# Second product of the MLP: another set of seven half-size products, with sums of the weights made in DRAM

## The chip, the cores and the metric

The program runs on one NeuronCore of a Trainium2 chip. The metric is device time in microseconds, from runs of the whole program; the profile comes from one more execution. TensorE multiplies, VectorE (DVE), ScalarE (ACT) and GpSimd (POOL) work on tiles of 128 partitions, and SyncE (SP) only issues DMA transfers.

## The reference

One layer of an encoder on 1024 tokens of width 1024 in float32: stick-breaking attention with 16 heads, an output projection and LayerNorm; cross-attention of 4 heads into 256 memory rows, a projection and LayerNorm; and a gated MLP:

```python
def conv_ffn(h, w_up, conv_w, conv_b, w_down):
    u = h @ w_up
    ch = u.shape[-1]
    u = lax.conv_general_dilated(u, conv_w, window_strides=(1,), padding=((CONV_W - 1, 0),),
                                 dimension_numbers=('NWC', 'WIO', 'NWC'), feature_group_count=ch) + conv_b
    g, val = jnp.split(u, 2, axis=-1)
    return (jax.nn.gelu(g) * val) @ w_down
```

`w_up` is 1024 x 5632 and `w_down` 2816 x 1024. A LayerNorm of 2^0.25 h plus this is the output. The change is in the last product, `@ w_down`.

## The kernel before

Each float32 matrix product is made of three TensorE products (`mm3`, L98 to L101): an operand x is kept as a high half, x rounded to the type float32r (a copy, most often on ScalarE, L77), and a low half, x minus that (a subtraction on VectorE, L83, or GpSimd, L85); high x high, high x low and low x high are added in a PSUM bank. `split` (L75) makes the halves.

The stages in order of time: attention with the q, k and v projections (to about 560 us), the first output projection and LayerNorm (`out_ln`, first loop of eight row blocks), cross-attention, the second output projection and LayerNorm (`out_ln`, second loop), the first product of the MLP with convolution and gate, whose gated rows are stored transposed in DRAM (`g_d`, 22 tiles of 128 channels x 1024 tokens), and the second product with the last LayerNorm.

At the very start x is loaded (`xT`, L392) in 16 pieces of 256 KB through two buffers (`sig`), split, and multiplied with the weights of the first head; `weights` (L162 to L168) loads and splits those of the next heads. In attention GpSimd makes low halves (L81, L85, L135, L136) and a mask (L217) that stands before VectorE's scan (L220).

The second product is cut in two along each of its three dimensions: tokens (th), channels (kh) and output columns (nh), so each quarter is 512 tokens x 1408 channels x 512 columns, with 11 = `NH` tiles of 128 channels. Seven half-size products replace the eight, from sums of the quarters (`plans`, L784 to L790): each product m has a sum of gated quarters and a sum of weight quarters. Products 2 and 4 run together, then 6 and 1, each pair in all eight banks, and then 3, 5, 7 one after the other in four banks each. For each of the 11 tiles `operands2` (L840) loads the blocks it needs, adds them on VectorE (L836), and splits them: the gated side with ScalarE and VectorE, the weight side with ScalarE and GpSimd. `plus` (L861) adds the finished banks and the residual into the output quarters; `finish` (L867) does a LayerNorm of 128 rows and stores them.

The program is written in one order, but a planner at build time (`schedule_with_timeline_sim=True`) sets the order of each engine's and queue's instructions; it keeps the dependencies through tiles and their buffers.

Of the kernel before, what the change touches and what calls it, by code (L numbers as in the profile page):

```python
# [19 lines left out]
F32 = mybir.dt.float32  # L20
# [15 lines left out]
NFF = 22  # L36
ALPHA = 2.0 ** 0.25
# [3 lines left out]
def trunk(ctx, tc, out, xT, xn, memT, wqk, wv, wo, xq, xk, xv, xo, up, cw, dn, lng, lnb):  # L41
# [17 lines left out]
    vm_d = dram.tile([P, 2, D], F32, name="vm_d")  # L59
    h1_d = [dram.tile([P, D], F32, name=f"h1_d{i}") for i in range(NTB)]  # L60
# [608 lines left out]
    with ExitStack() as c3:  # L669
# [3 lines left out]
        for i in range(NTB):  # L673
            out_ln(i, i, o2_d, wts2, h1_d, rp, gb, h2_d, h2_evac, first_products if i == NTB - 1 else None)
# [91 lines left out]
    for p in range(2, len(seq) - 1):  # L766
# [5 lines left out]
        else:  # L772
# [9 lines left out]

    NH = NFF // 2
    plans = {1: (("11", "22", ALU.add), ("11", "22", ALU.add)),  # L784
             2: (("21", "22", ALU.add), ("11",)),
             3: (("11",), ("12", "22", ALU.subtract)),
             4: (("22",), ("21", "11", ALU.subtract)),
             5: (("11", "12", ALU.add), ("22",)),
             6: (("21", "11", ALU.subtract), ("11", "12", ALU.add)),
             7: (("12", "22", ALU.subtract), ("21", "22", ALU.add))}  # L790
    with ExitStack() as c4:
        ea = c4.enter_context(pool(name="ea", bufs=1, reuse_waits="tile"))
        ep = c4.enter_context(pool(name="ep", bufs=1, reuse_waits="tile"))
        g_raw = {}

        def g_block(n, kt):
            th, kh = int(n[0]) - 1, int(n[1]) - 1
            if (n, kt) not in g_raw:
                if n == "21":
                    t = ea.tile([P, 512], F32, name="g21", bufs=NH + 2)  # L800
                elif n == "11":
                    if kt % 2 == 0:
                        g_raw["pair"] = ep.tile([P, 2, 512], F32, name="g11", bufs=6)
                    t = g_raw["pair"][:, kt % 2]
                else:
                    t = (ea if n == "22" and kt < 4 else ep).tile([P, 512], F32, name=f"g{n}_{kt}")
                g_raw[n, kt] = t
                nc.sync.dma_start(out=t, in_=g_d[NH * kh + kt][:, 512 * th:512 * th + 512])
            return g_raw[n, kt]

        w_kept, w_free = {}, []

        def w_blocks(ns, kt):

            ts = {}
            for n in ns:
                if n == "22":
                    if kt in w_kept:
                        ts[n] = w_kept[kt]
                        continue  # L820
                    t = w_kept[kt] = ea.tile([P, 512], F32, name="g21", bufs=NH + 2)
                else:
                    if not w_free:
                        pair = wrawp.tile([P, 2, 512], F32, name="wraw")
                        w_free.extend((pair[:, 0], pair[:, 1]))
                    t = w_free.pop(0)
                ts[n] = t
                kh, nh = int(n[0]) - 1, int(n[1]) - 1
                nc.sync.dma_start(out=t, in_=dn[NH * kh + kt][:, 512 * nh:512 * nh + 512])
            return ts  # L830

        def operand(plan, blocks, d, lo):
            x = blocks[plan[0]]
            if len(plan) > 1:
                t = ea.tile([P, 512], F32, name="sum", bufs=4)
# [155 lines left out]
```

## Time and profile before

| | us |
|---|---|
| median of 3 runs | 1615.63 (1611.7 to 1618.11) |
| the profiled execution | 1616.26 |
| its span, first to last instruction | 1614.5 |
| TensorE busy | 1524.7 (94%) |
| VectorE busy | 1162.7 (72%) |
| ScalarE busy | 705.2 (44%) |
| GpSimd busy | 730.4 (45%) |
| mean granted clock of TensorE | 0.984 |

All times of the rows are microseconds from the first instruction of that execution. PE is TensorE's matmuls, PEld its weight loads, SPq the DMA issues of SyncE. A matmul's own time of some 390 ns overlaps its neighbours'; what counts is how many there are in a stretch.

### The profile page before, as it was taken

What the parts mean: (1) busy time and instruction counts of PE and PEld (TensorE: products, weight loads), DVE (VectorE), ACT (ScalarE), POOL (GpSimd) and SP (SyncE); (2) the same over time, 40 slices, a digit from 0 to 9 for tenths busy, and PEclk for the clock granted to TensorE, in tenths of its full rate; (3) what the DMA queues carried; (4) which work ended last, traced back from release to release, by engine and by line L of the source; (5) the groups of instructions that cost most, each with busy time, mean ns of one, the idle gap of its engine ahead of it and who ended that gap; (6) DMA issues with size and microseconds to landing.
All of it is one profiled execution on the core that took longest, in us unless ns stands there. A gap on an engine that the chain in (4) does not pass through costs nothing.

```text
span 1614.5 us, 20972 instructions
## 1 busy us (share of the span) xinstructions
PE 1524.7 (94%) x7508; PEld 1262.0 (78%) x7508; DVE 1162.7 (72%) x1494; ACT 705.2 (44%) x1320; POOL 730.4 (45%) x604
## 2 busy tenths in 40 slices
PE   7999999999988999999999799999999998998975
PEld 5888888888877888888888577888888886866753
DVE  3466666666689556564467898777777778899998
ACT  4554655655676411233322444444444444433432
POOL 5865565656577601465002333232322234445584
PEclk9999999999999999999999999999999999999988
DMA  5322222222247433243253122222222216743221
GB/s 168 93 56 63 64 55 63 69 56 61 65 136 231 133 117 126 97 129 110 68 182 125 54 92 79 86 88 87 79 80 90 79 60 241 281 146 121 72 88 69
DMA packets 86520, 167.93 MB, mean 104 GB/s; under 512 B 10000, under 2 KB 31632, under 8 KB 86416
## 3 DMA queue, kind: packets, MB, share of 16 engines
q1 hardware_dynamic: 78352, 148.76, 29.0%
q10 hardware_dynamic: 8064, 17.83, 3.4%
q8 instruction: 59, 0.97, 0.3%
q14 instruction: 45, 0.37, 0.1%
HBM read 123.56 MB, written 34.60 MB: 98 GB/s over the span
## 4 chain that ended last, share of the span: by engine, by line
PE 71%; DVE 14%; issue 4%; DMA 4%; POOL 4%; ACT 2%; SPq 1%; DVEq 0%; POOLq 0%; ACTq 0%
PE yacc L99 4%; PE yacc L100 4%; PE yacc L101 4%; PE tp L229 3%; PE qkacc L101 3%; PE qkacc L99 3%; PE qkacc L100 3%; PE mb L99 3%; PE mb L101 3%; PE mb L100 3%; DVE sum L836 3%; PE ma L99 2%; PE ma L100 2%; PE mc L101 2%; PE mc L99 2%
## 5 line engine op out<-in xcount | busy, mean ns | idle before, releaser
L85 POOL TENSOR_TENSOR whl<-wraw,whl 128x512 fp32r<-128x512 f32 (+2 forms) x108 | 189.4, 1764 | 188.9 <-ACT whl L77 186.1
L220 DVE TENSOR_TENSOR_SCAN sig<-sig 128x896 f32<-128x896 f32 (+7 forms) x128 | 196.2, 1539 | 74.8 <-POOL sig L217 53.8
L83 DVE TENSOR_TENSOR wT<-tp,wT 128x512 fp32r<-128x512 f32 (+1 forms) x160 | 98.9, 629 | 64.2 <-ACT wT L77 63.1
L77 ACT CAST wT<-tp 128x512 fp32r<-128x512 f32 (+1 forms) x160 | 86.5, 545 | 104.9 <-PE tp L229 100.9
L100 PE MATMUL y<-whl,aop 128*128 128x512 f32 x292 | 118.1, 407 | 12.9 <-POOL whl L85 12.7
L101 PE MATMUL y<-whl,aop 128*128 128x512 f32 x292 | 114.8, 400 | 4.4 <-DVE aop L83 4.4
L99 PE MATMUL mb<-b_t,ws 128*128 128x512 f32 x264 | 105.0, 398 | 10.2 <-ACT ws L77 8.2
L215 ACT ACTIVATE sig<-z 128x384 f32<-128x384 f32 (+2 forms) x192 | 92.1, 496 | 51.4 <-PE z L214 50.2
L217 POOL TENSOR_SCALAR_AFFINE_SELECT sig<-sig 128x128 f32<-128x128 f32 x128 | 59.1, 466 | 119.5 <-ACT sig L215 111.8
L85 POOL TENSOR_TENSOR whl<-sum,whl 128x512 fp32r<-128x512 f32 x51 | 83.1, 1642 | 66.4 <-ACT whl L77 64.0
L99 PE MATMUL qkacc<-xh,whl 128*128 128x512 f32 x256 | 102.8, 402 | 8.2 <-POOL whl L85 5.6
L99 PE MATMUL y<-whl,aop 128*128 128x512 f32 x292 | 93.4, 405 | 11.8 <-ACT whl L77 6.6
L101 PE MATMUL mb<-b_t,ws 128*128 128x512 f32 x264 | 103.9, 395 | 0.0
L100 PE MATMUL mb<-b_t,ws 128*128 128x512 f32 x264 | 103.8, 393 | 0.0
L101 PE MATMUL qkacc<-xh,whl 128*128 128x512 f32 x256 | 101.1, 396 | 1.8 <-POOL whl L85 1.8
L100 PE MATMUL qkacc<-xl,whl 128*128 128x512 f32 x256 | 101.3, 396 | 0.0
L100 PE MATMUL yacc<-wo,whl 128*128 128x512 f32 x256 | 100.9, 394 | 0.0
L99 PE MATMUL yacc<-wo,whl 128*128 128x512 f32 x256 | 100.5, 393 | 0.3 <-ACT whl L77 0.3
L101 PE MATMUL yacc<-wo,whl 128*128 128x512 f32 x256 | 100.6, 394 | 0.0
L229 PE MATMUL tp<-ident,sig 128*128 128x128 f32 x576 | 89.4, 275 | 9.3 <-DVE wT L83 9.3
L77 ACT CAST ws<-wt 128x512 fp32r<-128x512 f32 x88 | 54.3, 620 | 93.3 <-PE mb L101 49.6
L81 POOL TENSOR_SCALAR whl<-wraw 128x512 fp32r<-128x512 f32 (+2 forms) x74 | 54.8, 753 | 88.0 <-PE qkacc L101 32.1
(224 smaller groups left out, 4416.3 us busy)
## 6 DMA issues: line engine op xcount, KB each, us to landing
wraw<-in_dn SPq DMA_DIRECT2D x66, 256.0 KB, 3.0
wraw<-in_up SPq DMA_DIRECT2D x22, 512.0 KB, 3.7
wr<-in_up SPq DMA_DIRECT2D x22, 512.0 KB, 3.5
g_d<-gate SPq DMA_DIRECT2D x22, 512.0 KB, 2.6
g<-g_d SPq DMA_DIRECT2D x44, 256.0 KB, 5.4
q<-q SPq DMA_DIRECT2D x64, 128.0 KB, 2.2
h_d<-r SPq DMA_DIRECT2D x32, 256.0 KB, 2.1
wraw<-in_wqk SPq DMA_DIRECT2D x15, 512.0 KB, 3.6
```

The lines of the kernel that those rows point to most:

```text
L77: nc.scalar.copy(out=hi, in_=src)
L81: nc.gpsimd.tensor_scalar(out=hi, in0=src, scalar1=1.0, scalar2=0.0, op0=ALU.mult, op1=ALU.add)
L83: nc.vector.tensor_tensor(out=lo, in0=src, in1=hi.bitcast(F32), op=ALU.subtract)
L85: nc.gpsimd.tensor_tensor(out=lo, in0=src, in1=hi.bitcast(F32), op=ALU.subtract)
L99: nc.tensor.matmul(o, lhsT=lh, rhs=rh, start=first, stop=False, skip_group_check=more)
L100: nc.tensor.matmul(o, lhsT=lh, rhs=rl, start=False, stop=False, skip_group_check=more)
L101: nc.tensor.matmul(o, lhsT=ll, rhs=rh, start=False, stop=last, skip_group_check=more)
L215: nc.scalar.activation(out=sig[:, a:b], in_=z[:, :b - a], func=AF.Sigmoid, scale=-0.125)
L217: nc.gpsimd.affine_select(out=sig[:, S - P:S], in_=sig[:, S - P:S], pattern=[[-1, P]], base=-1, channel_multiplier=1, compare_op=ALU.is_ge ...
L220: nc.vector.tensor_tensor_scan(out=kr, data0=kr, data1=kr, initial=1.0, op0=ALU.mult, op1=ALU.bypass)
L229: nc.tensor.transpose(out=tp[:, k], in_=sigs[2 * d + u][:, P * j:P * j + P], identity=ident)
L836: nc.vector.tensor_tensor(out=t, in0=x, in1=blocks[plan[1]], op=plan[2])
```

## The change

The second product uses another scheme of seven products with four sums on each side. With A for the gated quarters (first index tokens, second channels) and B for the weights' (channels, columns), the weights' sums are u1 = B11 + B12, u3 = B22 + B12, u2 = B22 + u1, u4 = B21 + u2. They are not made in SBUF: `u_steps` first copies 44 blocks of 256 KB from DRAM to DRAM on SyncE's queue, and then adds 44 blocks into them with accumulating transfers issued by GpSimd. Its steps are written six after each row block of the first output projection, and six before each of the second.

The gated quarters are loaded once into tiles of their own (`slot`, 4 x 11 blocks) and summed in place. The products come one by one, 1, 6, 2, 7, 5, 4, in two sets of four banks that alternate; products 2, 7 and 4 go on in banks that hold an earlier product. Each factor has its high half from ScalarE and its low half from VectorE. During products 5 and 4 the halves for the last product (slot 2 and B22) are made and kept, and that product is run row block by row block at the end with a LayerNorm behind each; the four LayerNorms of the other token half don't depend on it.

The diff, without the lines that it removes from the second product's stage (they are in the kernel above):

```diff
@@ -34,6 +34,7 @@
 M = 256
 XH = 4
 NFF = 22
+NH = NFF // 2
 ALPHA = 2.0 ** 0.25
 EPS = 1e-5
@@ -57,6 +58,7 @@
     o2_d = [[dram.tile([P, n, P], F32, name=f"o2_d{i}_{n}") for n in (6, 2)] for i in range(NTB)]
     km_d = [dram.tile([P, M], F32, name=f"km_d{i}") for i in range(KT)]
     vm_d = dram.tile([P, 2, D], F32, name="vm_d")
+    u_d = {n: [dram.tile([P, 512], F32, name=f"{n}_d{i}") for i in range(NH)] for n in ("u1", "u2", "u3", "u4")}
     h1_d = [dram.tile([P, D], F32, name=f"h1_d{i}") for i in range(NTB)]
     h2_d = [dram.tile([P, D], F32, name=f"h2_d{i}") for i in range(NTB)]
@@ -409,6 +411,23 @@
         pass
+    def b_block(n, kt):
+        kh, nh = int(n[0]) - 1, int(n[1]) - 1
+        return dn[NH * kh + kt][:, 512 * nh:512 * nh + 512]
+    def u_steps():
+        for n, x in (("u1", "11"), ("u3", "22"), ("u2", "22"), ("u4", "21")):
+            for kt in range(NH):
+                nc.sync.dma_start(out=u_d[n][kt], in_=b_block(x, kt))
+                yield
+        for n, x in (("u1", "12"), ("u3", "12"), ("u2", "u1"), ("u4", "u2")):
+            for kt in range(NH):
+                nc.gpsimd.dma_start(out=u_d[n][kt], in_=u_d[x][kt] if x[0] == "u" else b_block(x, kt),
+                                    accum_op=ALU.add, max_dma_last_dim=2048)
+                yield
     def load_ln(p, n):
         g = p.tile([P, D], F32, name="lng", bufs=1)
         b = p.tile([P, D], F32, name="lnb", bufs=1)
@@ -481,11 +500,14 @@
     def h1_evac(i, c, tp):
         split(tp, h1h[:, 4 * c:4 * c + 4, P * i:P * i + P], h1l[:, 4 * c:4 * c + 4, P * i:P * i + P])
+    u_sums = u_steps()
     with ExitStack() as c1:
         lnp = c1.enter_context(pool(name="ln1", bufs=1, side="right", reuse_waits="tile"))
         gb = load_ln(lnp, 0)
         for k, i in enumerate((4, 5, 2, 3, 0, 1, 6, 7)):
             out_ln(k, i, o_d, wts, xn, state["rp"], gb, h1_d, h1_evac)
+            for _ in range(6):
+                next(u_sums, None)
     mem_c.close()
@@ -671,6 +693,8 @@
         rp = c3.enter_context(pool(name="rp2", bufs=2, reuse_waits="tile"))
         gb = load_ln(lnp, 1)
         for i in range(NTB):
+            for _ in range(6):
+                next(u_sums, None)
             out_ln(i, i, o2_d, wts2, h1_d, rp, gb, h2_d, h2_evac, first_products if i == NTB - 1 else None)
@@ -780,176 +804,140 @@
...
+    plan = {1: (0, "11"), 6: (0, "u2"), 2: (2, "21"), 7: (None, "u3"), 5: (1, "u1"), 4: (3, "u4")}
     with ExitStack() as c4:
         ea = c4.enter_context(pool(name="ea", bufs=1, reuse_waits="tile"))
         ep = c4.enter_context(pool(name="ep", bufs=1, reuse_waits="tile"))
...
+        rs = [ep.tile([P, D], F32, name=f"y{i}") for i in range(NTB)]
+        slots = {}
+        def room(kt, s, dt):
+            return (ea if kt < 5 else ep).tile([P, 512], dt, name=f"{dt.name}{s}_{kt}", tag=f"g{s}_{kt}", bufs=1)
+        def slot(kt, s):
+            if (kt, s) not in slots:
+                t = slots[kt, s] = room(kt, s, F32)
+                nc.sync.dma_start(out=t, in_=g_d[NH * (s // 2) + kt][:, 512 * (s % 2):512 * (s % 2) + 512])
+            return slots[kt, s]
+        w_free = []
+        def w_block(n, kt):
+            if not w_free:
+                pair = wrawp.tile([P, 2, 512], F32, name="wraw")
+                w_free.extend((pair[:, 0], pair[:, 1]))
+            t = w_free.pop(0)
+            nc.sync.dma_start(out=t, in_=u_d[n][kt] if n[0] == "u" else b_block(n, kt))
+            return t
         def rows(n):
             th, nh = int(n[0]) - 1, int(n[1]) - 1
             return [(4 * th + b, slice(512 * nh, 512 * nh + 512)) for b in range(4)]
...
         quarters = {n: [rs[i][:, ns] for i, ns in rows(n)] for n in ("11", "12", "21", "22")}
...
+        c11, c12, c21, c22 = (quarters[n] for n in ("11", "12", "21", "22"))
+        def residual(n, b, x, op=ALU.add):
             i, ns = rows(n)[b]
...
+            t = ea.tile([P, 512], F32, name="h2r", bufs=2)
             nc.sync.dma_start(out=t, in_=h2_d[i][:, ns])
...
+            nc.vector.scalar_tensor_tensor(out=quarters[n][b], in0=t, scalar=ALPHA, in1=x, op0=ALU.mult, op1=op)
+        def add(d, x, y):
+            nc.vector.tensor_tensor(out=d, in0=x, in1=y, op=ALU.add)
+        def finish(i, spread):
+            layer_norm((rs[i][:, 0:512], rs[i][:, 512:1024]), *gb, spread=spread)
             for n in range(2):
                 ns = slice(512 * n, 512 * n + 512)
                 (nc.scalar if n else nc.sync).dma_start(out=out[i, :, ns], in_=rs[i][:, ns])
...
+        def factors(m, kt):
+            s, n = plan[m]
+            if m == 6:
+                nc.vector.tensor_tensor(out=slot(kt, 0), in0=slot(kt, 1), in1=slot(kt, 0), op=ALU.subtract)
+            if m == 7:
+                x = ea.tile([P, 512], F32, name="sum", bufs=2)
+                nc.vector.scalar_tensor_tensor(out=x, in0=slot(kt, 0), scalar=-1.0, in1=slot(kt, 3),
+                                               op0=ALU.mult, op1=ALU.subtract)
+            else:
+                x = slot(kt, s)
+            w = w_block(n, kt)
+            a = ea.tile([P, 2, 512], R, name="aop", bufs=4)
+            if kt % 2 == 0:
+                two["w"] = whlp.tile([P, 2, 2, 512], R, name="whl")
+            return (x, (a[:, 0], a[:, 1])), (w, (two["w"][:, kt % 2, 0], two["w"][:, kt % 2, 1]))
+        two = {}
+        def down(bank, b, a, w, first, last, more):
             bb = slice(P * b, P * b + P)
...
+            mm3(bank, a[0][:, bb], a[1][:, bb], w[0], w[1], first, last, more)
+        banks = ([f(name="ya") for f in (acc_tile, acc_tile, pv_tile, pv_tile)],
+                 [f(name="yb") for f in (z_tile, z_tile, tp_tile, tp_tile)])
+        last_ops = [[None, None] for _ in range(NH)]
+        gb = None
+        for n, m in enumerate((1, 6, 2, 7, 5, 4)):
+            y = banks[n % 2]
+            more = m in (2, 7, 4)
+            if m == 5:
+                y = banks[0][:] = [f(name="ya") for f in (acc_tile, acc_tile, pv_tile, pv_tile)]
             for kt in range(NH):
...
+                ops = factors(m, kt)
+                for x, d in ops:
+                    split(x, *d)
+                a, w = ops[0][1], ops[1][1]
+                for b in range(4):
+                    down(y[b], b, a, w, kt == 0 and not more, kt == NH - 1, more)
+                if m == 1:
+                    nc.vector.tensor_tensor(out=slot(kt, 1), in0=slot(kt, 1), in1=slot(kt, 3), op=ALU.subtract)
+                if m == 2:
+                    add(slot(kt, 2), slot(kt, 2), slot(kt, 0))
+                if m == 5:
+                    t = w_block("22", kt)
+                    wo = room(kt, 0, R), room(kt, 1, R)
+                    split(t, *wo)
+                    last_ops[kt][1] = wo
                     if 3 <= kt < 7:
...
+                        residual("22", kt - 3, c22[kt - 3], ALU.subtract)
+                if m == 4:
+                    vo = room(kt, 3, R), room(kt - 1, 2, R) if kt else ea.tile([P, 512], R, name="vl")
+                    split(slot(kt, 2), *vo)
+                    last_ops[kt][0] = vo
+                    if 3 <= kt < 7:
+                        residual("21", kt - 3, c21[kt - 3])
                     elif kt >= 7:
...
+                        residual("12", kt - 7, c12[kt - 7], ALU.subtract)
+            if m == 7:
+                gb = load_ln(ep, 2)
             for b in range(4):
...
+                if m == 1:
+                    nc.scalar.copy(out=c21[b], in_=y[b])
+                elif m == 6:
+                    add(c12[b], y[b], c21[b])
+                elif m == 2:
+                    residual("11", b, y[b])
+                elif m == 7:
+                    add(c22[b], y[b], c21[b])
+                elif m == 5:
+                    add(c22[b], c22[b], y[b])
                 else:
...
+                    add(c21[b], c21[b], y[b])
+        for b in range(4):
             for kt in range(NH):
...
+                a, w = last_ops[kt]
+                down(banks[0][b], b, a, w, False, kt == NH - 1, True)
+            finish(4 + b, b < 3)
+            add(c12[b], c12[b], banks[0][b])
+            finish(b, b % 2 == 0)
 def kernel(**inputs):
```

## Rows read from the trace of the kernel before

**Rows 1.** Windows: in the first product, all of the second, 40 us of it.

```profile
1060.00:1100.00 40.00, 40.00 (x175) 32.61 (x174) 30.45 (x37) 18.21 (x24) 11.03 (x6) 1.00 0.23 79
1336.00:1615.00 279.00, 230.44 (x938) 178.11 (x936) 255.94 (x296) 104.15 (x182) 152.19 (x99) 0.94 0.42 143
1420.00:1460.00 40.00, 34.97 (x144) 25.87 (x142) 39.28 (x45) 13.08 (x23) 16.19 (x12) 1.00 0.47 143
```

**Rows 2.** Timeline: start us, us, engine, line, operation, names; first and last.

```profile
1336.58 0.50 PE L99 MATMUL y<-whl,aop 128*128 128x512 f32 x1 [0.22 <-ACT aop L77]
...
1596.75 0.39 PE L101 MATMUL y<-g,aop 128*128 128x512 f32 x1
...
1609.47 1.40 DVE L441 SCALAR_TENSOR_TENSOR y<-y,rs,lnb 128x512 f32<-128x512 f32 x2
```

**Rows 3.** Waits from 1338 us: total us, times, longest.

```profile
POOL whl L85 <- ACT whl L77: 101.3, 36, 11.2
ACT aop L77 <- DVE sum L836: 76.0, 27, 6.2
...
PE y L100 <- POOL whl L85: 12.7, 13, 3.1
```

**Rows 4.** Durations ns, min/median/max, of VectorE's operations in the second product.

```profile
L836 DVE TENSOR_TENSOR sum<-g,g x55: 636/680/1783, 1334.9 to 1586.1; 128x512 f32<-128x512 f32 x55
...
L863 DVE TENSOR_TENSOR y<-y,y x24: 632/674/692, 1426.3 to 1597.6; 128x512 f32<-128x512 f32 x24
L865 DVE SCALAR_TENSOR_TENSOR y<-sum,y x16: 669/1775/1798, 1424.4 to 1531.6; 128x512 f32<-128x512 f32 x16
```

**Rows 5.** Timeline within the second product.

```profile
1421.45 0.62 ACT L77 CAST aop<-sum 128x512 fp32r<-128x512 f32 x1 [3.62 <-DVE sum L836]
...
1422.67 2.99 POOL L85 TENSOR_TENSOR whl<-sum,whl 128x512 fp32r<-128x512 f32 x2 [2.40 <-ACT whl L77]
1422.84 1.68 DVE L836 TENSOR_TENSOR sum<-g,g 128x512 f32<-128x512 f32 x1
...
1426.86 0.68 DVE L836 TENSOR_TENSOR sum<-wraw 128x512 f32<-128x512 f32 x1
...
1427.46 0.68 DVE L83 TENSOR_TENSOR aop<-sum,aop 128x512 fp32r<-128x512 f32 x1
```

**Rows 6.** Timeline of SyncE's queue: loads of the second product.

```profile
1371.75 5.53 SPq L808 DMA_DIRECT2D g<-g_d  x9
1377.65 0.33 SPq L415 DMA_DIRECT2D lng<-in_lng  x1
```

**Rows 7.** Windows: the two output projections, the start, and attention.

```profile
561.00:660.00 99.00, 99.00 (x464) 81.98 (x464) 60.06 (x99) 14.85 (x22) 14.54 (x12) 1.00 0.36 119
820.00:905.00 85.00, 82.10 (x384) 67.28 (x383) 65.83 (x109) 25.75 (x45) 17.98 (x14) 0.99 0.38 130
0.00:30.00 30.00, 23.15 (x90) 17.79 (x91) 12.03 (x17) 11.21 (x17) 11.80 (x23) 1.00 0.65 210
30.00:60.00 30.00, 27.13 (x121) 21.18 (x120) 7.87 (x7) 14.33 (x28) 26.56 (x27) 1.00 0.31 88
100.00:150.00 50.00, 50.00 (x282) 42.80 (x281) 30.87 (x36) 27.77 (x62) 34.67 (x35) 1.00 0.27 75
```

**Rows 8.** Timeline of SyncE's queue at the start; landing of the x loads.

```profile
15.89 0.33 SPq L164 DMA_DIRECT2D wraw<-in_wqk  x1
...
17.89 7.12 SPq L392 DMA_DIRECT2D sig<-in_xT  x4
...
DMA to landing us min/median/max: 2.5/3.8/7.1
```

**Rows 9.** Timeline of ScalarE and GpSimd in attention.

```profile
129.13 0.20 ACT L148 COPY vend<-vT 128x4 f32<-128x4 f32 x1
...
129.85 0.12 POOL L144 MEMSET vT<- 128x1 f32 x1
```

**Rows 10.** Page, DMA issues: KB each, median us from issue to landing.

```profile
g<-g_d SPq DMA_DIRECT2D x44, 256.0 KB, 5.4
```

More of the change, by code (lines that the diff above doesn't have):

```diff
@@ L778, in trunk @@
     b4c.close()
[L783 to L790, printed above, removed]
+    plan = {1: (0, "11"), 6: (0, "u2"), 2: (2, "21"), 7: (None, "u3"), 5: (1, "u1"), 4: (3, "u4")}
     with ExitStack() as c4:
@@ L793, in trunk @@
         ep = c4.enter_context(pool(name="ep", bufs=1, reuse_waits="tile"))
[L794 to L835, printed above, removed]
-                nc.vector.tensor_tensor(out=t, in0=x, in1=blocks[plan[1]], op=plan[2])
-                x = t
-            split(x, d[:, 0], d[:, 1], "act", lo)
-        def operands2(ms, kt, a, w):
-            need = [sorted({n for m in ms for n in plans[m][s] if isinstance(n, str)}) for s in range(2)]
-            gs, ws = {n: g_block(n, kt) for n in need[0]}, w_blocks(need[1], kt)
-            for k, m in enumerate(ms):
-                operand(plans[m][0], gs, a[k], "dve")
-                operand(plans[m][1], ws, w[k], "pool")
+        rs = [ep.tile([P, D], F32, name=f"y{i}") for i in range(NTB)]
@@ L849, in rows @@
             return [(4 * th + b, slice(512 * nh, 512 * nh + 512)) for b in range(4)]
-        rs = [ep.tile([P, D], F32, name=f"y{i}") for i in range(NTB)]
         quarters = {n: [rs[i][:, ns] for i, ns in rows(n)] for n in ("11", "12", "21", "22")}
-        def residual(n, b):
+        c11, c12, c21, c22 = (quarters[n] for n in ("11", "12", "21", "22"))
+        def residual(n, b, x, op=ALU.add):
             i, ns = rows(n)[b]
-            t = ea.tile([P, 512], F32, name="sum", bufs=4)
+            t = ea.tile([P, 512], F32, name="h2r", bufs=2)
             nc.sync.dma_start(out=t, in_=h2_d[i][:, ns])
-            return t
-        def plus(n, b, x, y, op=ALU.add, scale=None, eng=None):
-            if scale is None:
-                (eng or nc.vector).tensor_tensor(out=quarters[n][b], in0=x, in1=y, op=op)
-            else:
-                nc.vector.scalar_tensor_tensor(out=quarters[n][b], in0=x, scalar=scale, in1=y, op0=ALU.mult, op1=op)
-        def finish(i):
-            layer_norm((rs[i][:, 0:512], rs[i][:, 512:1024]), *gb, spread=i in (0, 1, 4, 6))
+            nc.vector.scalar_tensor_tensor(out=quarters[n][b], in0=t, scalar=ALPHA, in1=x, op0=ALU.mult, op1=op)
[3 more added lines that the diff above has]
+            layer_norm((rs[i][:, 0:512], rs[i][:, 512:1024]), *gb, spread=spread)
             for n in range(2):
@@ L883, in trunk @@
-        banks = [acc_tile, acc_tile, pv_tile, pv_tile, z_tile, z_tile, tp_tile, tp_tile]
-        for ms in ((2, 4), (6, 1)):
-            ys = [[f(name="y") for f in banks[4 * k:4 * k + 4]] for k in range(2)]
-            for kt in range(NH):
-                a, w = operand_tiles()
-                operands2(ms, kt, a, w)
-                for k in range(2):
-                    for b in range(4):
-                        down(ys[k], b, a[k], w[k], kt)
-                if ms == (6, 1):
-                    if 3 <= kt < 7:
-                        b = kt - 3
-                        plus("22", b, residual("22", b), c21[b], ALU.subtract, ALPHA)
-                        plus("21", b, c21[b], c11[b])
+        def factors(m, kt):
[13 more added lines that the diff above has]
+            return (x, (a[:, 0], a[:, 1])), (w, (two["w"][:, kt % 2, 0], two["w"][:, kt % 2, 1]))
```

59 lines of the change are left out of this document (removed).

## The prediction

> **What bounds the kernel now.** I read the windows first, to find the stage that the change rewrites and what it lacks. Up to about 1336 us the first product of the MLP keeps TensorE full: 40.00 us busy in 40, 175 matmuls of 512 columns, so one per 0.2286 us [rows 1]. In the second product TensorE falls to 34.97 us in 40 while VectorE stands at 39.28, and over the whole of it VectorE is busy 255.94 us of 279 [rows 1]. The timeline gives the ends: the second product's first matmul starts at 1336.58 us, its last ends at 1597.14, and the last LayerNorm instruction ends at 1610.87, 3.6 us before the span of 1614.5 is over [rows 2]. This stage holds 7 products x 11 k-tiles x 4 row blocks x 3 = 924 matmuls and the 12 last ones of the first product. At 0.2286 us these 936 need 214.0 us; they took 260.5. So 46.5 us are lost inside the stage, and 17.4 us lie between the last matmul and the end of the span. That is all the change can win here.
>
> The waits say why: GpSimd waited 101.3 us for ScalarE and ScalarE 76.0 us for VectorE's sums, and TensorE's longest sum of waits is on GpSimd [rows 3]. VectorE is not full of work but of waiting for GpSimd: the same 128x512 sum takes 0.68 us at the median and 1.78 at most, and the residual's 1.78 at the median where 0.67 is the least [rows 4]. The timeline shows when: two GpSimd splits ran from 1422.67 to 1425.66, and the sum that VectorE started beside them took 1.68 us; once GpSimd was idle, VectorE took 0.68 us an operation and started one every 0.60 [rows 5].
>
> **The stage after the change.** GpSimd gets no split and no addition any more; it keeps the power of each LayerNorm and the products of five of them. VectorE gets 11 x (12 low halves of the six products + 4 sums + 2 low halves kept for the last product) = 198 operations. At 0.60 us each [rows 5] that is 119 us; 20 additions of banks at 0.67 are 13 and 16 residuals at 0.67 are 11 [rows 4]. Together 143 us, beside the 792 matmuls of the first six products, 181 us. A single product needs at most 33 x 0.60 + 8 x 0.67 + 4 x 0.67 = 28 us of VectorE against 132 x 0.2286 = 30.2 us of TensorE. ScalarE has 154 high halves at 0.62 us [rows 5], 95 us. So TensorE becomes the bound, and two bank sets give every evacuation a whole product of time.
>
> Not all of the 46.5 us come back. The first product's loads are four blocks of 256 KB a k-tile (three of gated rows, one of weights). The queue issued nine such loads in 5.53 us [rows 6], so a k-tile takes about 2.5 us of loading and 2.74 us of matmuls: just enough, with no reserve, and the rows from k-tile 5 on wait for buffers that the first product of the MLP frees, as the loads of this row did, sent at 1371.75 us. I leave 8 us lost (bounds 3 and 14: nothing but the first operands, or the whole of this row's load time paid twice). The tail: after the last matmul come one addition, one LayerNorm and the store. Four LayerNorms that do not wait for the last product and three that do are done under its 30 us of matmuls; a LayerNorm is at most six operations of VectorE on 512 columns, 4.1 us at 0.68, so seven and the additions are up to 32 us, and VectorE may end a little late. I take 13 us in place of 17.4 (bounds 9 and 17). Gain of the stage: 46.5 - 8 + 4.4 = 43 us, bounds 33 to 51.
>
> **The 44 copies and 44 accumulating transfers.** They are written beside the two output projections, where the DMA engines are 0.36 and 0.38 busy and TensorE is full or nearly so [rows 7]. There 44 copies at 0.61 us would fill 27 us of 184 and cost nothing; TensorE's work in these 184 us hides them, and if that cover were gone the price would be those 27 us. But they would have to stay there. They read weights that lie in DRAM from the start, and no buffer holds them back. The trace shows what happens to such work: queues are not filled in the order of the program. The weights of the second head were issued at 15.89 us, ahead of the last loads of the x that the first head still needs [rows 8]. The last LayerNorm's scale was fetched at 1377.65 us, in the middle of the first pair of products, though it is written after the second pair [rows 6]. A GpSimd memset ran at 129.85 us, right after the copy that ended at 129.33 and freed its buffer, and well ahead of its user [rows 9]. Each went as soon as its buffer was free. A copy that needs no buffer is free at 0 us.
>
> So I expect the 44 copies in the gaps of SyncE's queue in the first 40 us, and the accumulating transfers on GpSimd soon behind them. There the gaps exist (the four loads at 17.89 us spread over 7.12 us, with a buffer awaited between them [rows 8]), but the loads are on the path: x comes in through two buffers, so after the first two k-tiles there are three rounds, each waiting for its buffer and then for its load, and TensorE is already working (23.15 us of the first 30 [rows 7]). A full queue has a load land 5.4 us after its issue at the median, with issues 0.61 us apart, about eight in flight [rows 6, 10]. The x loads landed after 3.8 us [rows 8]. With copies in front, each round pays 5.4 - 3.8 plus 0.6 for its place: 2.2 us if copies go at the pace of loads, and at half that pace (they read and write DRAM, which no row shows) 10.8 - 3.8 + 1.2 = 8.2. Three rounds: 7 to 25 us; I take 16, the middle.
>
> The Trainium skill, "DMA: Bandwidth & Descriptors", section Latency and other measured facts, has DRAM-to-DRAM copies at up to 214 GB/s a direction; by that, 256 KB takes 1.2 us (an estimate), the half pace, and the price would be the upper 25 us rather than 16.
>
> GpSimd's part: it is busy 26.56 us of the 30 between 30 and 60 us, and 34.67 of 50 later [rows 7]. Behind an accumulating transfer stand its splits of q and k and the mask before VectorE's scan, and so the transposes on TensorE. No row has such an issue; the nearest are GpSimd's own, from 0.12 us (a memset [rows 9]) to 1.5 (a split [rows 5]). Hidden in its idle time it costs 0, at 44 x 1.5 all on the path 66. I take 9: a dozen fall where GpSimd is full, at 0.75 us. Later ones lie under TensorE's 50.00 us in 50. Price together 25 us, bounds 0 and 91.
>
> **Sum.** 1614.5 - 43 + 25 = 1596.5 us of span. The profiled execution took 1616.26, 1.8 more than its span and 0.6 more than the median of the runs, so the run should take about 1598 us.
>
> **The rivals.**
> *The copies cost nothing* (they stay at the projections, or the start has room): 1616.3 - 43 = 1573 us, 1565 to 1583. For it speaks that the DMA engines are only 0.65 busy in the first 30 us [rows 7]; against it [rows 8] and [rows 9].
> *The accumulating transfers hold GpSimd, and the kernel gets slower.* GpSimd's queue is in order: a transfer that has to wait for its copy, or for the one before it, stops the masks and splits of attention behind it. Place: 15 to 200 us. It decides once they put more than 43 - 16 = 27 us on the path, 0.6 us for each of the 44. At one 1.5 us operation each, 66 us, the run takes 1616.3 - 43 + 16 + 66 = 1655 us; at two thirds of that, 1633. For it: GpSimd has 3 us free between 30 and 60. Against: TensorE is full at 100 to 150 us although GpSimd is 0.69 busy [rows 7], so there is slack.
> The Trainium skill, "SBUF — State Buffer", section SBUF: two separate sides, warns of just this engine: transfers issued by GpSimd are held up while VectorE has the port that they share. By its figures, 3.1 us in place of 0.62, the 44 would take 136 us of GpSimd; no run here shows one yet.
> *VectorE stays the bound* (its operations stay at 1.0 us without GpSimd beside them): 198 + 25 + 8 LayerNorms of 4 us is 255 us, as much as now [rows 1]; gain 5, and with the 25 us of the start 1636 us. Against it stand the 0.60 us steps of [rows 5].
>
> **How the numbers follow.** My forecast (gain 33 to 51, price 12 to 40) has 0.50 and lies within 1578 and 1620, about 1598. Free copies 0.28; GpSimd's block 0.15; VectorE 0.07. A change of 0.5%, 8 us, is about what a measurement of this kernel tells from none: 1607.5 and 1623.7 are the bounds. Faster: 0.36 of my case, all 0.28, 0.01 of the rest, 0.65. Same: 0.13 and 0.05, 0.18. Slower: 0.01 and 0.16, 0.17. The range runs from inside the free case to the mild end of the block, 1566 to 1628.
>
> **What would show it.** Right: no GpSimd split and VectorE at 0.68 us in the last 280 us, TensorE at 39 us or more in 40, the last LayerNorm alone behind the last matmul; copies on SyncE's queue before 45 us, x landing later than 7 us, TensorE idle there by some 15 us more. Wrong: copies beside the projections (then near 1573), TensorE waiting for rows or weights in the stage, or attention stretched by GpSimd.

## Result: slower by 1.3%, and the profile after

The changed kernel takes 1636.43 us (median of 4 runs, 1633.92 to 1641.42) against 1615.78 before: ratio 1.0134, 95% interval 1.0103 to 1.0166. The profiled execution's span is 1634.6 us, 20.1 more than before. The forecast was 1598.

The stage that was rewritten did what it should. Windows of the changed kernel (us, then busy time and count of PE, PEld, DVE, ACT, POOL, the granted clock, the busy share of the DMA engines, GB/s): the start, then the whole second product and its first part.

```profile
0.00:30.00 30.00, 19.13 (x72) 14.40 (x72) 9.84 (x13) 8.72 (x13) 15.81 (x28) 1.00 0.90 270
30.00:60.00 30.00, 14.62 (x39) 10.04 (x40) 5.53 (x8) 8.53 (x17) 17.44 (x22) 0.61 1.09 277
60.00:100.00 40.00, 17.43 (x68) 13.73 (x67) 0.69 (x1) 5.91 (x10) 23.07 (x25) 0.71 1.09 253
100.00:150.00 50.00, 41.03 (x215) 34.45 (x216) 32.78 (x27) 22.31 (x50) 40.95 (x44) 0.85 0.63 143
1393.00:1635.00 242.00, 217.84 (x948) 178.86 (x948) 186.73 (x300) 98.61 (x166) 19.93 (x18) 0.96 0.49 163
1400.00:1420.00 20.00, 12.34 (x55) 9.84 (x53) 16.45 (x21) 5.41 (x7) 0.00 (x0) 0.89 0.64 219
1420.00:1440.00 20.00, 18.01 (x71) 14.74 (x72) 15.81 (x26) 8.43 (x15) 0.00 (x0) 0.85 1.00 353
```

Its timeline: the second product's first and last matmul, and VectorE's last work.

```profile
1392.91 0.50 PE L101 MATMUL ya<-whl,aop 128*128 128x512 f32 x1 [0.49 <-ACT aop L79]
...
1621.32 0.39 PE L103 MATMUL ya<-float32r,float32r 128*128 128x512 f32 x1
...
1630.03 1.41 DVE L460 SCALAR_TENSOR_TENSOR y<-y,rs,lnb 128x512 f32<-128x512 f32 x2
```

From its first matmul to the end of the span the second product takes 241.7 us, where it took 277.9 [rows 2]: 36.2 us won. But that first matmul starts at 1392.91 us and not at 1336.58 [rows 2]: 56.3 us lost before it, and 56.3 - 36.2 is the 20.1. The loss lies in the first 130 us. From 60 to 100 us TensorE did 68 matmuls; in a kernel without the sums' transfers (below) it did 230. TensorE's granted clock fell too while it stood: 0.61, 0.71 and 0.85 in the three stretches after 30 us (1.00 is the upper of its two levels, 2.4 GHz, and 0.50 the lower, 1.2 GHz), so some of its work between the waits ran at the lower one; without the transfers the same stretches have 0.94, 1.00 and 1.00.

The view of DMA issues has the sums' transfers (KB each, median us to landing); under it TensorE's waits in the first 150 us (us in all, times, longest):

```profile
u_d<-in_dn SPq DMA_DIRECT2D x44, 256.0 KB, 13.1
...
u_d<-in_dn POOLq DMA_DIRECT2D x22, 256.0 KB, 10.7
u_d<-u_d POOLq DMA_DIRECT2D x22, 256.0 KB, 13.0
```

```profile
PE z L216 <- DMA q<-q: 31.1, 1, 31.1
PE qkacc L101 <- ACT xh L79: 19.7, 6, 9.0
```

And the chain that ends at 140 us, in order of time (start, us, what):

```profile
17.27 11.07 DMA wraw<-in_wv
28.36 11.74 DMA u_d<-in_dn
40.12 10.57 DMA u_d<-in_dn
50.70 16.89 DMA u_d<-in_dn
67.61 18.23 DMA u_d<-in_dn
85.86 14.15 DMA u_d<-in_dn
100.07 8.32 DMA q<-q
```

The chain runs from copy to copy: a copy on SyncE's queue is issued when an older one has landed, and the loads of x and of weights and the q moves stand in the same queue. The DMA engines' share is 0.90 to 1.09 for 100 us on end.

### The profile page after: what moved, and what is told of

The parts are those of the page before. It is cut to its first block, busy times and chain, and to the rows that moved or that the text cites. A ratio compares the mean times of both kernels' runs of the same rounds, so it can differ in the third digit from the quotient of the medians.

```text
span 1634.6 us, 20991 instructions
## 1 busy us (share of the span) xinstructions
PE 1520.0 (93%) x7508; PEld 1266.1 (77%) x7508; DVE 1099.9 (67%) x1500; ACT 700.7 (43%) x1306; POOL 639.4 (39%) x565
## 4 chain that ended last, share of the span: by engine, by line
PE 76%; DMA 9%; DVE 9%; issue 2%; POOL 2%; ACT 2%; SPq 0%; DVEq 0%; POOLq 0%; ACTq 0%
DMA u_d<-in_dn 4%; PE yacc L101 4%; PE yacc L102 4%; PE yacc L103 4%; PE mb L101 3%; PE mb L103 3%; PE mb L102 3%; PE tp L231 3%; PE qkacc L101 3%; PE qkacc L102 3%; PE qkacc L103 3%; PE ma L101 2%; PE ma L102 2%; PE ma L103 2%; PE mc L101 2%
## 5 line engine op out<-in xcount | busy, mean ns | idle before, releaser
L222 DVE TENSOR_TENSOR_SCAN sig<-sig 128x896 f32<-128x896 f32 (+7 forms) x128 | 204.2, 1603 | 90.7 <-POOL sig L219 51.4
L87 POOL TENSOR_TENSOR whl<-wraw,whl 128x512 fp32r<-128x512 f32 (+2 forms) x97 | 178.5, 1856 | 155.9 <-ACT whl L79 154.7
L446 POOL TENSOR_TENSOR rs<-rs,mhalf 128x1 f32<-128x1 f32 x24 | 21.3, 890 | 362.4 <-DVE rs L445 362.4
L79 ACT CAST whl<-wraw 128x512 fp32r<-128x512 f32 (+3 forms) x113 | 82.2, 739 | 108.2 <-PE yacc L103 33.1
L101 PE MATMUL qkacc<-xh,whl 128*128 128x512 f32 x256 | 104.9, 410 | 21.8 <-ACT xh L79 19.7
L103 PE MATMUL qkacc<-xh,whl 128*128 128x512 f32 x256 | 103.2, 403 | 4.6 <-POOL whl L87 4.6
L216 PE MATMUL z<-k,q 128*128 128x384 f32 (+2 forms) x192 | 68.6, 359 | 31.1 <-DMA q<-q 31.1
L83 POOL TENSOR_SCALAR whl<-wraw 128x512 fp32r<-128x512 f32 (+2 forms) x74 | 62.3, 871 | 79.8 <-PE q2acc L103 23.1
L85 DVE TENSOR_TENSOR whl<-wraw,whl 128x512 fp32r<-128x512 f32 (+3 forms) x90 | 66.4, 746 | 35.0 <-ACT whl L79 34.8
## 6 DMA issues: line engine op xcount, KB each, us to landing
u_d<-in_dn SPq DMA_DIRECT2D x44, 256.0 KB, 13.1
```

Of the source, the lines that this page charges most:

```text
L79: nc.scalar.copy(out=hi, in_=src)
L83: nc.gpsimd.tensor_scalar(out=hi, in0=src, scalar1=1.0, scalar2=0.0, op0=ALU.mult, op1=ALU.add)
L85: nc.vector.tensor_tensor(out=lo, in0=src, in1=hi.bitcast(F32), op=ALU.subtract)
L87: nc.gpsimd.tensor_tensor(out=lo, in0=src, in1=hi.bitcast(F32), op=ALU.subtract)
L101: nc.tensor.matmul(o, lhsT=lh, rhs=rh, start=first, stop=False, skip_group_check=more)
L103: nc.tensor.matmul(o, lhsT=ll, rhs=rh, start=False, stop=last, skip_group_check=more)
```

## The experiments

The transfers' price is measured against e2_no_sums, which has none: 1581.73 us. Runs of one kernel lie up to some 7 us off their median, so a few us between single runs (e2 to e6, e9, e11) mean nothing.

| run | us | over e2_no_sums |
|---|---|---|
| the change | 1636.43 | 54.7 |
| e1_late | 1620.42 | 38.7 |
| e2_no_sums | 1581.73 | 0 |
| e3_copies_only | 1592.67 | 10.9 |
| e4_half | 1617.05 | 35.3 |
| e5_88_copies | 1595.85 | 14.1 |
| e6_pool_plain | 1630.42 | 48.7 |
| e7_ffn | 1634.10 | 52.4 |
| e8_adds_late | 1994.18 | 412 |
| e9_thin_adds | 1615.14 | 33.4 |
| e10_ffn_lag | 1606.85 | 25.1 |
| e11_adds_2nd | 1626.99 | 45.3 |
| e12_spread | 1583.97 | 2.2 |
| e13_bulk_early | 1584.70 | 3.0 |

**1. Is it the start?** In e1_late a few elements of each sum's block are first written from a row block that the first output stage has just finished, so its copy can't go earlier.

```diff
+                nc.sync.dma_start(out=u_d[n][kt][0:1, 0:8], in_=u_after["d"][0:1, 0:8])
                 nc.sync.dma_start(out=u_d[n][kt], in_=b_block(x, kt))
...
             out_ln(k, i, o_d, wts, xn, state["rp"], gb, h1_d, h1_evac)
+            u_after["d"] = h1_d[i]
```

> Each of the 44 copies waits for a row that the first output stage has written, so no sum can start before that stage; everything else is as after the change. Theory A (the 44 copies and 44 accumulating transfers fill the transfer engines in the first 130 us and hold up the start; the rest of the change gives what it does in the profile after): the start is as before, 56 us come back, 1575 to 1585 us. Theory B (the transfers cost their time wherever they are, or the later stages were moved for another reason): 1605 or more. By the forecast's own price for the start (25 us), 1611.

e2_no_sums reads plain blocks and issues none of the 88 transfers; e3_copies_only leaves the second loop of u_steps out; e4_half moves 256 of the 512 columns and reads plain blocks as e2_no_sums does.

```diff
-            nc.sync.dma_start(out=t, in_=u_d[n][kt] if n[0] == "u" else b_block(n, kt))
+            nc.sync.dma_start(out=t, in_=b_block({"u1": "12", "u2": "22", "u3": "22", "u4": "21"}.get(n, n), kt))
...
-    u_sums = u_steps()
+    u_sums = iter(())
```

> No sums in DRAM at all: the four products that want a sum read one plain weight block in its place, so the transfers in the second product are as many and as large as after the change (left out: the sums themselves). Theory A: 1575 to 1582 us, the start is that of before and the second product stays at some 242 us. Theory B: the same as e1_late only if the transfers cost nothing in the output stages; if they cost there too, e2_no_sums is faster than e1_late by what they cost.

> The 44 plain copies stay at the start, the 44 accumulating transfers on GpSimd's queue are left out (so the sums are not made). If the price of the start goes by bytes moved, about half of the 56 us stays, 20 to 30: 1600 to 1610 us. If it is SyncE's queue, where copies stand ahead of loads and of the q transfers, 40 or more stay: 1618 or more. If it is GpSimd and its queue, under 12 stay: under 1592.

> All 44 copies and 44 accumulating transfers at the start, each with half of the columns (128 x 256 in place of 128 x 512); the second product reads plain blocks as in e2_no_sums (left out: the sums). If bytes set the price of the start, about half of it goes, or more: 1595 to 1610 us. If the number of transfers, their waits in the queues or GpSimd's issue set it, nearly all of it stays: 1625 or more.

e1_late took 1620.42 us (ratio to before 1.0032, 1.0017 to 1.0047), so theory A fell: the price came along to the output stages. e2_no_sums shows that the rest of the change is worth what its profile showed. Windows of e2_no_sums, then of e3_copies_only:

```profile
60.00:100.00 40.00, 40.00 (x230) 34.37 (x229) 26.46 (x30) 20.40 (x46) 25.83 (x26) 1.00 0.21 64
1336.00:1580.00 244.00, 219.54 (x948) 179.20 (x948) 186.91 (x300) 98.41 (x166) 19.93 (x18) 0.96 0.48 161
```

```profile
30.00:60.00 30.00, 27.85 (x117) 21.64 (x117) 5.13 (x8) 13.20 (x25) 21.51 (x22) 0.95 1.01 331
```

With copies alone the engines are as full (1.01) and move more (331 GB/s), TensorE does 117 matmuls where it did 39, and the copies land after 6.1 us and not 13.1. So a full set of DMA engines is not the price by itself, and the copies cost 10.9 us of the 54.7. The accumulating transfers on top cost 43.8. Half the bytes of both left 35.3: the price goes neither by bytes alone nor by number alone.

Waits of e1_late from 561 to 830 us show another place where time went:

```profile
POOL u_d L429 <- DMA u_d<-in_dn: 64.1, 11, 11.2
...
DVE r L463 <- POOL rs L449: 26.3, 6, 8.0
```

GpSimd stood 64 us before accumulating transfers whose copies were still on their way, and VectorE 26 us for the power of a LayerNorm that stood behind them.

**2. Bytes or GpSimd?** The same bytes as plain copies, on either queue, into tiles of their own:

```diff
-        for n, x in (("u1", "12"), ("u3", "12"), ("u2", "u1"), ("u4", "u2")):
+        for n, x in (("u1", "12"), ("u3", "12"), ("u2", "11"), ("u4", "22")):
             for kt in range(NH):
-                nc.gpsimd.dma_start(out=u_d[n][kt], in_=u_d[x][kt] if x[0] == "u" else b_block(x, kt),
-                                    accum_op=ALU.add, max_dma_last_dim=2048)
+                nc.sync.dma_start(out=v_d[n][kt], in_=b_block(x, kt))
```

(e6_pool_plain has nc.gpsimd in the last line.)

> The 44 copies as after the change, and in place of the 44 accumulating transfers 44 more plain copies of weight blocks of the same size into other DRAM tiles, on SyncE's queue too (left out: the sums). Nothing on GpSimd. Bytes theory (a plain transfer of 256 KB costs the start what an accumulating one costs): 1615 to 1630 us. GpSimd theory (the accumulating transfers' waits on GpSimd's queue, or their own slowness, make the 44 us that e3_copies_only did not have): 1595 to 1606, two to three times the 11 us of e3_copies_only.

> As e5_88_copies, with the 44 further plain copies on GpSimd's queue in place of SyncE's; none of them waits for a copy of the first 44 (left out: the sums). If GpSimd's waiting for the copies, or the accumulation, makes the price: near e5_88_copies, under 1610 us. If it is issuing from GpSimd as such, or its kind of transfer: 1620 or more.

44 more copies on SyncE's queue cost 3 us, which is within the scatter; the same 44 on GpSimd's queue cost 38, nearly as much as accumulating ones, though they wait for no copy. GpSimd's timeline in e6_pool_plain, and two rows of its DMA issues:

```profile
41.09 0.52 POOL L427 DMA_DIRECT2D vu_d<-in_dn  x1 [0.62 <-DMA vu_d<-in_dn]
...
54.94 0.52 POOL L427 DMA_DIRECT2D vu_d<-in_dn  x1 [0.72 <-DMA u_d<-in_dn]
55.49 0.63 POOL L84 TENSOR_SCALAR whl<-wraw 128x512 fp32r<-128x512 f32 x1
```

```profile
u_d<-in_dn SPq DMA_DIRECT2D x44, 256.0 KB, 10.9
vu_d<-in_dn POOLq DMA_DIRECT2D x44, 256.0 KB, 9.3
```

Each issue takes 0.52 us, but before nearly each GpSimd waits until an earlier transfer of its own has landed (the copy of SyncE's that the row at 54.94 us names can't be it: this transfer needs none): from 29 to 55 us it does nothing else, and its split of the weights comes at 55.49. More of the price is on SyncE's side: in the first 150 us TensorE waited 7.6 us for a split of GpSimd's and 25.6 us for halves of x. The loads of x took up to 18.7 us to land, 6.6 in e5_88_copies, and SyncE's copies land after 10.9 us, 6.3 in e5_88_copies. The DMA queues from 30 to 60 us (packets, MB, share of the 16 engines; q1 has SyncE's transfers and q0 GpSimd's), first of e5_88_copies, then of e6_pool_plain:

```profile
q1 hardware_dynamic: 5158, 9.84, 98.2%
```

```profile
q0 software_dynamic: 2011, 6.59, 65.2%
q1 hardware_dynamic: 2084, 3.81, 37.0%
```

The two queues get through nearly the same number of packets, and SyncE's moves 3.81 MB where it moved 9.84. The Trainium skill, "DMA: Bandwidth & Descriptors", section SWDGE vs HWDGE vs iDMA, says that inside each DMA engine the queue of transfers issued by GpSimd and those of the other issuers are served in turn; the nearly equal counts of packets agree.

e9_thin_adds takes the bytes away and leaves the number and the waits:

```diff
-                nc.gpsimd.dma_start(out=u_d[n][kt], in_=u_d[x][kt] if x[0] == "u" else b_block(x, kt),
+                nc.gpsimd.dma_start(out=u_d[n][kt][:, 0:64],
+                                    in_=(u_d[x][kt] if x[0] == "u" else b_block(x, kt))[:, 0:64],
```

> As after the change, copies and accumulating transfers at the start, but each accumulating transfer adds 64 of the 512 columns (left out: the rest of the sums). If GpSimd's waiting for SyncE's copies makes the price, it stays above 1618 us. If it is the time that the accumulating transfers themselves take (their bytes, and the places in flight that they hold), nearly all of the 44 us goes: 1590 to 1600.

1615.14 us, between the two: 22.5 us over e3_copies_only. Its copies land after 6.7 us, hardly later than in e3_copies_only, so these 22.5 are not SyncE's queue; they point at GpSimd. In the first 130 us the 44 issues themselves kept GpSimd for 37.7 us, and it stood 12.4 us before them (39.1 and 31.0 in the changed kernel). How much of the 22.5 is issuing and how much is standing no run separates.

The other 21.3 us of the 43.8 come with the bytes. The queues of the changed kernel from 60 to 100 us:

```profile
q0 software_dynamic: 2565, 4.66, 65.1%
q1 hardware_dynamic: 3001, 5.44, 43.4%
```

SyncE's queue moves 5.44 MB in 40 us, 136 GB/s, where it moved 331 GB/s with copies alone.

**3. In a stage with room.** e7_ffn issues copies and accumulating transfers block by block in the MLP's first product, tied to its gated rows as e1_late ties them:

```diff
         stage3(w)
+        if w.half:
+            u_after["d"] = g_d[w.j]
+            for _ in range(10):
+                next(u_sums, None)
```

> All sums made, but each copy waits for a gated row of the MLP's first product, and the copies and accumulating transfers go block by block, 10 transfers for each second pair of that stage (445 us long, transfer engines 0.25 busy, GpSimd 0.30). Bytes theory: they fit there, 1578 to 1588 us, faster than both kernels. GpSimd theory (whoever stands behind the accumulating transfers on GpSimd waits for the copies, wherever they are): GpSimd makes the second halves of the weights there, so 1595 to 1620.

1634.10 us (ratio 1.0111, 1.0076 to 1.0146), above both expectations. The second product starts at 1391 us, so nearly all is lost in this stage. A window, and waits of GpSimd and VectorE (1010 to 1391 us):

```profile
1050.00:1350.00 300.00, 273.48 (x1128) 216.12 (x1126) 213.56 (x227) 107.87 (x145) 104.73 (x74) 0.97 0.49 130
```

```profile
POOL u_d L428 <- DMA u_d<-in_dn: 122.0, 26, 20.5
...
POOL u_d L428 <- DMA u_d<-u_d: 30.8, 8, 5.6
```

```profile
DVE wt L629 <- POOL ws L87: 44.9, 9, 9.3
```

The DMA engines are half idle and GpSimd only a third busy, yet it stands 153 us at transfers whose copy, or whose earlier sum, has not landed. Behind them stand the splits of the next weights, for which VectorE waits 44.9 us, up to 9.3 at a time (16.0 and 1.3 before the change). Before the change GpSimd waited for no transfer in this stage.

**4. Where GpSimd has nothing else to do.** e8_adds_late and e11_adds_2nd copy most rows of each block in the MLP's first product and the last rows near its end, so that all accumulating transfers run in the second product. They differ in the cut: 127 and 1 rows, or 112 and 16.

```diff
-                nc.sync.dma_start(out=u_d[n][kt], in_=b_block(x, kt))
+                nc.sync.dma_start(out=u_d[n][kt][1:P], in_=b_block(x, kt)[1:P])
```

In e11_adds_2nd, with a and b 0 and 112, two k-tiles at a time (rows 112 to 128 go later, in one transfer for the 11 tiles of each sum):

```diff
+        nc.sync.dma_start(out=u_all[n][a:a + 1, ks, 0:8], in_=d[0:1, 0:w].rearrange("p (k c) -> p k c", c=8))
+        nc.sync.dma_start(out=u_all[n][a:b, ks], in_=blocks(SRC[n][0], ks)[a:b])
```

> All sums made. The copies (all but one row of each block) wait for gated rows of the MLP's first product; the last row waits for a gated row near that stage's end, and so the accumulating transfers run in the second product, where GpSimd has nothing else to do for 200 us. GpSimd theory (what stands behind the transfers on GpSimd's queue is late, and that alone makes the price): no stage waits any more, 1580 to 1592 us, faster than both kernels. Bytes theory (the transfer engines' time makes the price): the second product's own loads are in the way, 1600 to 1625.

> As e8_adds_late, with the copies cut at 112 and 16 rows in place of 127 and 1: copies in the MLP's first product, all 44 accumulating transfers in the second one, where GpSimd has nothing else to do. Bytes theory: the first product is as before the change (its second product starts at 1336 to 1340 us), and the second one is held up by full transfer engines for 44 x 2 us: 1610 to 1630. GpSimd theory alone: 1582 to 1592.

e8_adds_late failed as an experiment: its first product alone is some 370 us longer. SyncE's timeline there:

```profile
1046.80 14.38 SPq L426 DMA_DIRECT2D u_d<-in_dn  x3
1061.28 10.03 SPq L626 DMA_DIRECT2D wr<-in_up  x1
```

The issues of three copies of 127 rows took 14.38 us together, and that of the load behind them 10.03. The DMA queue from 1046 to 1071 us:

```profile
q1 hardware_dynamic: 288, 0.57, 6.0%
```

That is the time of about one engine of 16. The Trainium skill, "DMA: Bandwidth & Descriptors", section Why a DMA increments its semaphore by 16 and not by 1, says that 127 partitions put all of a transfer on one engine; this agrees, and with 112 and 16 rows the second product starts at 1331.5 us.

e11_adds_2nd then answers the question: 1626.99 us, all of the loss in the second product. A window, GpSimd's timeline, what its transfers took to land (min/median/max, 1376 to 1420 us), and the DMA queues from 1380 to 1420 us:

```profile
1400.00:1420.00 20.00, 7.45 (x21) 5.09 (x19) 5.87 (x9) 4.74 (x9) 8.12 (x10) 0.69 1.10 266
```

```profile
1378.50 0.81 POOL L447 DMA_DIRECT2D u_d<-in_dn  x1 [1.19 <-DMA u_d<-in_dn]
1380.51 0.81 POOL L447 DMA_DIRECT2D u_d<-in_dn  x1 [1.20 <-DMA u_d<-in_dn]
```

```profile
DMA to landing us min/median/max: 15.8/15.8/17.0
```

```profile
q0 software_dynamic: 2837, 5.16, 69.9%
q1 hardware_dynamic: 2837, 5.39, 40.4%
```

One every 2.01 us, with 15.8 / 2.01 = 8 in flight, for 80 us, while the engines are full (1.06 to 1.11). The accumulating transfers alone don't fill them: 69.9% of 2.01 us is 1.4 us of all engines for each. But they take packet for packet with the loads, equal counts, so the loads get 5.39 MB in 40 us, 135 GB/s. The chain of work of this stretch runs over three loads of gated rows and one of a sum, which took 12.2, 16.1, 16.1 and 17.3 us to land; before these it stands some 12 us (1352.9 to 1364.7) at SyncE's copies of the last rows. Nobody waits for GpSimd here. So there are two prices, and the turn that GpSimd's transfers take from loads that are needed makes most of the 45 us here.

**5. Both hidden.** e10_ffn_lag goes back to the MLP's first product, but the last 16 rows of a block come a step after the rest and only then its accumulating transfer, u2's and u4's one step later each. e13_bulk_early moves the copies of 112 rows to the two output stages; e12_spread also spreads what remains over all pairs.

```diff
+    def u_step(q, d):
+        for lag, ns in ((1, ("u1", "u3")), (2, ("u2",)), (3, ("u4",))):
+            if 0 <= q - lag < 6:
+                ks = [rows_after(d, n, q - lag, 112, 128) for n in ns][0]
+                for n in ns:
+                    for kt in ks:
+                        x = SRC[n][1]
+                        nc.gpsimd.dma_start(out=u_d[n][kt], in_=u_d[x][kt] if x[0] == "u" else b_block(x, kt),
+                                            accum_op=ALU.add, max_dma_last_dim=2048)
...
         stage3(w)
+        if w.half:
+            u_step((p - 3) // 2, g_d[w.j])
```

In e12_spread and e13_bulk_early three copies behind each row block of the output stages (h2_d[i] in the second), and in e12_spread a step with one k-tile for every pair:

```diff
             out_ln(k, i, o_d, wts, xn, state["rp"], gb, h1_d, h1_evac)
+            bulk_step(h1_d[i])
...
         stage3(w)
+        u_step(p - 3, g_d[w.j] if w.half else gate[0])
```

> All sums made, in the MLP's first product as in e7_ffn, but no accumulating transfer waits for a transfer just issued: 112 of a block's 128 rows are copied one pair of pairs ahead, the last 16 rows of u1 and u3 a step later, of u2 two and of u4 three steps later, and the accumulating transfers come behind these. GpSimd theory (its standing at a transfer whose input is still on its way made e7_ffn's 55 us): 1583 to 1595 us, faster than both kernels. Bytes theory (2 us of all transfer engines for each accumulating transfer): the stage has room for it, the same. If GpSimd's issuing or the software queue as such holds the stage up: 1610 or more.

> Only the copies moved, as in e12_spread; the last rows and the accumulating transfers stay as in e10_ffn_lag, eight for every second pair. If the copies on SyncE's queue made the rest of the loss: as e12_spread, under 1597 us. If it is the accumulating transfers' bursts: 1600 to 1608.

> As e10_ffn_lag, with the copies of 112 rows moved to the two output stages (three behind each row block, none on GpSimd's way), and the last rows and accumulating transfers spread over all pairs of the MLP's first product, four for each pair of some 20 us. If what e10_ffn_lag still lost (23 us in that stage) came of bursts in which copies and accumulating transfers stand before the loads of the up weights: 1585 to 1597 us. If it is the 88 us of the transfer engines or the issuing on GpSimd, wherever they stand: 1603 to 1612 as e10_ffn_lag.

e10_ffn_lag: 1606.85 us, ratio 0.9947 (0.9926 to 0.9968), between its two expectations, with 23 us still lost in that stage. GpSimd still stands 42.8 us at copies there, but VectorE waits only 6.8 us for its splits. Another wait of VectorE says where the time goes (1010 to 1336 us):

```profile
DVE wt L642 <- DMA wr<-in_up: 42.2, 5, 12.2
```

The up weights stood behind bursts of copies. With the copies moved this wait is gone: e13_bulk_early takes 1584.70 us (0.9814, 0.9797 to 0.9831) and e12_spread 1583.97 (0.9803, 0.9768 to 0.9838). Both make every sum, beat both kernels, and are within 3 us of the kernel without sums. e12_spread's windows and GpSimd's wait:

```profile
1010.00:1100.00 90.00, 90.00 (x393) 73.32 (x392) 72.36 (x81) 40.36 (x52) 38.55 (x31) 1.00 0.53 127
1100.00:1336.00 236.00, 235.61 (x1022) 191.34 (x1021) 200.11 (x208) 104.61 (x138) 94.56 (x65) 1.00 0.49 123
```

```profile
POOL u_d L443 <- DMA u_d<-in_dn: 45.3, 17, 8.9
```

The DMA share is that of e7_ffn (0.49) and TensorE is full. GpSimd still stands 45 us, now where nothing urgent is behind it: VectorE waits 8.3 us for its splits, up to 2.6 at a time.

## Why the forecast was wrong

**Right: the transfers run to the front.** Copies were issued from 9.6 us on, accumulating transfers from 16.4 on. They lasted longer than said: copies to 96.9 us and not 45. The x loads landed after 5.0 us at the median and 12.9 at most, 3.8 and 7.1 before [rows 8].

**Right, a little too high: the stage.** 36.2 us against 43 (33 to 51; the terms at their best, 46.5 - 3 + 8.4, give 52). The tail is 12.9 us (1621.7 to 1634.6), forecast 13. Inside, 948 matmuls x 0.2286 are 216.7 us of 228.8: 12.1 lost where 8 were forecast, nearly all (11.2 by its 126 matmuls) between 1400 and 1440 us, where TensorE waited 10.1 us for halves of gated rows, whose loads ran at 219 and then 353 GB/s, and its granted clock was 0.89 and 0.85. VectorE left the bound as forecast: 186.73 us of 242, GpSimd 19.93 in place of 152.19 [rows 1], and VectorE's low halves took 0.69 us.

**Right in size, in part by luck: the copies.** 10.9 us alone (two single runs), forecast 16 (7 to 25). The forecast put all of it on the rounds of x; TensorE waited 9.6 us for halves of x in e3_copies_only and 6.9 in e2_no_sums, so that explains some 3 us of it, and the rest was lost later.

**The step that failed: GpSimd's part, "I take 9: a dozen fall where GpSimd is full, at 0.75 us".** Measured 43.8 us, inside its bounds of 0 to 66 and five times the value taken. The duration was about right: in the profile after an issue takes 0.81 us (from in_dn) or 1.33 (from u_d) at the median, and 0.81 for both in e7_ffn and e11_adds_2nd. What failed is that only a dozen would be on the path, at their duration alone. The 44 issues hold GpSimd for 39.1 us of the first 130, and it stands 31.0 us more before them, because an issue that may not go yet holds GpSimd until its copy has landed and one of its own earlier transfers has; with an eighth of the bytes 22.5 us were left. The bytes were not in the term at all: GpSimd's transfers take turns with SyncE's in the DMA engines, so that SyncE's copies land after 13.1 us and the loads and q moves between them wait. In e3_copies_only a full set of engines had cost little. Nor was TensorE's lower clock while it waits in any term.

**The rivals.** "The accumulating transfers hold GpSimd, and the kernel gets slower" (0.15) is what happened, at its lower end (1633 to 1655 against 1636). Its mechanism is half of it; it left out the turns in the DMA engines, so its good number is in part luck. The Trainium skill's page that was cited with it, "SBUF — State Buffer", section SBUF: two separate sides, gives that figure for a whole transfer beside a copy on VectorE and was read as 3.1 us of GpSimd an issue; the 0.81 and 1.33 us here do not bear that reading out, 47 us for 44 in place of 136. "The copies cost nothing" is near e2_no_sums, 1573 forecast and 1581.73 measured. "VectorE stays the bound" gave 1636 for a wrong reason. The forecast's aside that beside the output stages the copies would cost nothing holds for copies (e13_bulk_early); for copies and accumulating transfers together it does not (e1_late).

Open: how the 43.8 us at the start split exactly, since the causes feed each other there (issuing, standing, SyncE's late transfers, and TensorE's lower clock while it waits), and how much of e1_late's 38.7 and e7_ffn's 52.4 is GpSimd's standing and how much SyncE's copies in bursts, which cost e10_ffn_lag some 22.

## What to carry to other kernels

A transfer has two prices besides its bytes: what stands behind it in its issuer's queue, and the turn that it takes in the DMA engines from another queue's loads. On an engine that also computes, ask of each issue what it may have to wait for (its source, an earlier transfer's place) and what stands behind; a busy share of a third and half-idle DMA engines did not keep e7_ffn from losing 52 us. Work without a buffer or an input to hold it goes wherever a queue has a gap, so tie it to data of the stage that has room, the input well ahead of its user, and spread.

## What the runs showed of the hardware that was not expected

- While GpSimd's queue had transfers, the DMA engines served it and SyncE's packet for packet (2837 and 2837 in e11_adds_2nd), and SyncE's moved 135 GB/s where it moved 331 without.
- Beside such loads accumulating DRAM-to-DRAM transfers of 256 KB went one every 2.01 us (130 GB/s of data added), 1.4 us of all DMA engines each; 88 plain copies of 256 KB on SyncE's queue beside the start's own loads cost 14 us in all.
- GpSimd had 8 of its transfers in flight and stood at the next: issues of 0.81 us came 2.01 us apart.
- Plain transfers of 256 KB cost 3 us for 44 on SyncE's queue and 38 on GpSimd's (single runs).
- Copies of 127 rows ran at 6.0% of 16 engines and held the issue of the load behind them for 10.03 us; 112 and 16 rows in e11_adds_2nd left that stage as long as before the change.
